# Issuing the attention scores of two key heads together, alternating between the lower and upper 64 rows

## The chip, the cores and the metric

The kernel runs on one core of one Trainium2 chip. Its metric is the device time of one execution in microseconds (us); lower is better. The program has two layers and is fully unrolled, so every instruction in the profile stands for one place in the code.

## The reference

A decoder trunk of two layers over 256 tokens and 2048 features, all in fp32. The part of a layer that the change touches is the attention half of its mixer: 16 query heads, 4 key heads of 64 features (four query heads share a key head), rotary positions, a window of 128 tokens and a sink value for each query head:

```python
q = rope(q.reshape(B, S, N_Q_HEADS, HEAD_DIM), positions)
k = rope(k.reshape(B, S, N_KV_HEADS, HEAD_DIM), positions)
...
# sliding_window_attention, blocks of 128 tokens, own and previous block as keys
scores = einsum('bnqhgd,bnkhd->bnhgqk', qb, kk) * HEAD_DIM ** -0.5
scores = where(valid, scores, MASK_VALUE)
m = maximum(max(scores, -1), sink)
e = exp(scores - m)
probs = e / (sum(e, -1) + exp(sink - m))
out = einsum('bnhgqk,bnkhd->bnqhgd', probs, vv)
```

Beside it a layer has a gated recurrence (the other half of the mixer), an output projection, a gated feed forward of width 5632 and a gated per-layer embedding. All big products are products of the 256 tokens with weight matrices that are read once.

## The kernel before, in words

The 256 tokens are two token tiles t = 0 and 1 of 128. A weight matrix is walked in strips of 512 output columns (`strip`), and a strip in chunks of 256 rows: `load_w` (lines 185 to 193) reads a chunk with one DMA and splits it into a high part (ScalarE, line 159) and a low part (VectorE, line 160). A chunk is then 12 matmuls of 512 columns on TensorE, six for each token tile (lines 206, 207, 208: high by high, low by high, high by low). They accumulate in four PSUM banks of their own (`pacc`). Split weights have eight buffers, so the splits can run up to eight chunks ahead of TensorE.

Everything smaller is threaded between the chunks. After each chunk `tick` advances the generators that are under way (one `yield` to the next) and runs what `later(n, ...)` had put off by n chunks. What is traced in this way is a program order; the framework's planner makes the order of each engine's queue from it, taking the earliest instruction of the program whose inputs are there by its own estimate of time. A queue then runs in that order on the chip. The small work shares four PSUM banks (`ms`, taken with `bank()`) and six buffers of 128x512 (`nat`).

A layer's mixer begins with the strip of keys and values. `done_kv` (line 404) rotates the keys: VectorE multiplies (line 395), GpSimd adds and subtracts (line 402), and TensorE transposes the result two or three chunks later (`turn`, line 414) into `kT`, whose lower 64 partitions hold the even key head of a half and the upper 64 the odd one. Then come two strips of queries, a half of the heads each. When a strip of queries is done, `attend` starts for each token tile, t = 1 one chunk behind t = 0: after three chunks the rotated queries are transposed (line 434), and from then on the two key heads g = 0 and 1 of the half go through `head_group` in three steps each, a chunk apart, with head 1 one chunk behind head 0:

- scores: a product over 64 rows (`rows = g * 64 ...`) for each of four query heads, line 464 for the own block and, for t = 1, line 472 for the block before; then the softmax up to its exponentials (lines 468 to 487, VectorE and ScalarE);
- the transposes of the exponentials (line 491) and their masks (lines 494 to 498);
- the products with the values (lines 503 and 505) and the division.

The attention of a half so runs during the next strip. That of half 1 runs during the first strip of the recurrence; at its end the outputs are scaled and transposed (`split_T`, lines 167, 175, 176), close to the first transposes of the recurrence (line 531).

Of the kernel before, what the change touches and what calls it, by code (L numbers as in the profile page):

```python
# [15 lines left out]
P = 128  # L16
# [23 lines left out]
BIG = (25600.0, 134.0, 1.921875, 0.005126953125, 1.6254460206255317e-05)  # 4096 * 2 pi  # L40
TWO = (6.28125, 0.0019350051879882812, 3.0199157663446385e-07)  # 2 pi
ROUND = 12582912.0  # 1.5 * 2^23
# [3 lines left out]
def decoder(ctx: ExitStack, tc: tile.TileContext, x, p, positions, w_in, attn_sinks,  # L46
# [23 lines left out]
    def later(n, fn):  # L70
        """trace fn n weight chunks from now"""
        queue.append((clock[0] + n, fn))
# [3 lines left out]
    def start(gen):  # L76
        """trace gen up to its first yield, and from one yield to the next every chunk"""
        running.append(gen)
        if next(gen, True):
            running.remove(gen)  # L80
# [17 lines left out]
    xr = [[xp.tile([P, W], F32, tag=f"x{t}{s}", name=f"x{t}{s}") for s in range(4)]  # L98
          for t in range(NT)]
# [6 lines left out]
    # per-feature vectors, one feature per partition  # L106
# [28 lines left out]
    def rstd(ss, n, count=1, name="rs"):  # L135
        """(ss / n + eps) ^ -0.5, ss [P, count]"""
        v = tiny(count)
        V.tensor_scalar(v, ss, 1.0 / n, EPS, op0=ALU.mult, op1=ALU.add)
        r = sm.tile([P, count], F32, name=name)
        G.tensor_tensor(r, v, mhalf[:, 0:count], op=ALU.pow)  # L140
        return r
# [15 lines left out]
    def split(src, hi, lo):  # L157
        """src = hi + lo, each of at most 12 significant bits"""
        S.copy(hi, src)  # L159
        V.tensor_tensor(lo, src, hi.bitcast(F32), op=ALU.subtract)  # L160

    def split_T(src_blocks, gcols, hl, t, kt0=0):
        """transpose 128-wide blocks [tok, feat] and split, per-feature gain if given"""
        n = len(src_blocks)
        ps = bank((P, n, P))
        for b, blk in enumerate(src_blocks):
            T.transpose(ps[:, b], blk, ident)  # L167
        h = hl[0][:, kt0:kt0 + n, t * P:(t + 1) * P]
        lo = hl[1][:, kt0:kt0 + n, t * P:(t + 1) * P]
        if gcols is None:  # L170
            split(ps, h, lo)
            return
        for b in range(n):
            g = gcols[:, b:b + 1]
            S.activation(h[:, b], ps[:, b], AF.Copy, scale=g)  # L175
            V.scalar_tensor_tensor(lo[:, b], ps[:, b], g, h[:, b].bitcast(F32),  # L176
                                   op0=ALU.mult, op1=ALU.subtract)
# [7 lines left out]
    def load_w(w, c, col):  # L185
        """two k-tiles of 512 columns, split"""
        raw = wpr.tile([P, 2, W], F32, tag="wr", name="wr")
        nc.sync.dma_start(raw, w[c * 2 * P:(c + 1) * 2 * P, col:col + W].rearrange(
            "(k p) n -> p k n", p=P))
        hi = wps.tile([P, 2, W], F32R, tag="wh", name="wh")  # L190
        lo = wps.tile([P, 2, W], F32R, tag="wl", name="wl")
        split(raw, hi, lo)
        return hi, lo

    def strip(lhs, w, col, done, nch=8, row0=0, skew=0, psum=None, pre=None):
        """512 output columns for both token tiles; lhs[c] = (hi, lo) of 4 k-tiles"""
# [31 lines left out]
    def post_norm(mg, ss, t, nss, xT, gcols):  # L228
        """after the last strip of a token tile: x += mg * rstd, and the next input"""
        r = sum_rstd(ss[t], D, f"po{t}")  # L230
        for c in range(4):
            V.scalar_tensor_tensor(xr[t][c], mg[c][:, t], r[:, 0:1], xr[t][c],  # L232
                                   op0=ALU.mult, op1=ALU.add)
            next_in(t, c, xT, gcols)
        for c in range(4):
            square_sum(xr[t][c], nss[t][:, c:c + 1])
# [16 lines left out]
    # ---- masks, sinks and rotary tables  # L253
    ones = cp.tile([P, P], F32, name="ones")
    m_low = cp.tile([P, P], F32, name="m_low")      # [j, i]: i >= j
    m_up = cp.tile([P, P], F32, name="m_up")        # [j, i]: i < j
    m_prev = cp.tile([P, P], F32, name="m_prev")    # [i, j]: j > i
    m_neg = cp.tile([P, P], F32, name="m_neg")      # [i, j]: j > i gives the mask value
    LEV = (1, 2, 4, 8, 16, 32, 64)  # block lengths; the last two take no mask
# [11 lines left out]
    def constants():  # L271
# [15 lines left out]
        # lower bounds: softmax over the layers, cumulative sum minus the first  # L287
# [22 lines left out]
        # attention sinks, on every partition  # L310
# [4 lines left out]
        # rotary angles: token per partition  # L315
# [52 lines left out]
    for l in range(DEPTH):  # L368
        # ================= mixer =======================================================
# [20 lines left out]
        def rotate(src, tb, i, n, o1, o2):  # L390
            """src [P, n heads, 64] in PSUM; o1, o2: [P, n/4, 4, 32] views in the order (g, j)"""
# [12 lines left out]
        def done_kv(t, ps):  # L404
# [11 lines left out]
            later(3 - t, turn)  # L416
# [12 lines left out]
        def attend(half, t, o):  # L429
# [7 lines left out]
            two = [head_group(half, g, t) for g in range(2)]  # L437
            next(two[0])
            yield
            next(two[1])  # L440
            next(two[0])
            yield
            next(two[1])
            next(two[0], None)
            yield
            next(two[1], None)
# [9 lines left out]
        def head_group(half, g, t):  # L456
            """four query heads on one key head: scores; then the exponentials' transpose; then values"""
            kv = 2 * half + g
            rows = slice(g * 64, (g + 1) * 64)
            q = qT[half]  # L460
            hs = slice(kv * 4, kv * 4 + 4)
            pc = bank((P, 4, P))
            for j in range(4):
                T.matmul(pc[:, j], q[rows, j, t * P:(t + 1) * P], kT[rows, half, t * P:(t + 1) * P],  # L464
                         start=True, stop=True)
            s_ = nat((P, 4, P))
            if t == 0:
                V.tensor_tensor(s_, pc, m_neg.unsqueeze(1).to_broadcast([P, 4, P]), op=ALU.add)
            else:
                pp = bank((P, 4, P))  # L470
                for j in range(4):
                    T.matmul(pp[:, j], q[rows, j, t * P:(t + 1) * P],
                             kT[rows, half, (t - 1) * P:t * P], start=True, stop=True)
                S.copy(s_, pc)
                V.copy_predicated(s_, m_prev.bitcast(I32).unsqueeze(1).to_broadcast([P, 4, P]), pp)
            nm = tiny(4)
            V.tensor_reduce(nm, s_, axis=AX.X, op=ALU.max, negate=True)
            V.tensor_tensor(nm, nm, nsink[:, l, hs], op=ALU.min)  # L478
            den = tiny(4)
            for j in range(4):  # L480
                S.activation(s_[:, j], s_[:, j], AF.Exp, bias=nm[:, j:j + 1],  # L481
                             accum_out=den[:, j:j + 1])
            es = tiny(4)
            V.tensor_tensor(es, sink[:, l, hs], nm, op=ALU.add)
            S.activation(es, es, AF.Exp)
            V.tensor_tensor(den, den, es, op=ALU.add)
            V.reciprocal(den, den)
            yield
            pt = bank((P, 4, P))
            for j in range(4):  # L490
                T.transpose(pt[:, j], s_[:, j], ident)  # L491
            ec = nat((P, 4, P))
            if t == 0:
                S.copy(ec, pt)
            else:
                ep = nat((P, 4, P))
                V.tensor_tensor(ec, pt, m_low.unsqueeze(1).to_broadcast([P, 4, P]), op=ALU.mult)
                V.tensor_tensor(ep, pt, m_up.unsqueeze(1).to_broadcast([P, 4, P]), op=ALU.mult)
            yield
            po = bank((P, 4, 64))  # L500
            for j in range(4):
                if t > 0:
                    T.matmul(po[:, j], ep[:, j], vv[:, t - 1, kv * 64:(kv + 1) * 64],
                             start=True, stop=False)
                T.matmul(po[:, j], ec[:, j], vv[:, t, kv * 64:(kv + 1) * 64],  # L505
                         start=t == 0, stop=True)
            dst = ao[t][:, half, g * 256:(g + 1) * 256]
            V.tensor_tensor(dst.rearrange("p (j d) -> p j d", d=64), po,
                            den.unsqueeze(2).to_broadcast([P, 4, 64]), op=ALU.mult)
            square_sum(dst, ssa[t][:, kv:kv + 1], (P, 256))  # L510

        class Rec:
            """four heads of the gated recurrence"""
# [151 lines left out]
        # ---- output projection, post norm  # L665
# [17 lines left out]
        # ================= feed forward ================================================  # L683
# [50 lines left out]
        # ================= gated per-layer embedding ===================================  # L734
# [61 lines left out]
```

## Time and profile before

| | |
|---|---|
| Time, median of 3 runs | 2515.0 us (2514.89 to 2515.26) |
| Span of the profiled execution | 2514.3 us |
| TensorE matmuls busy | 2490.2 us, 99% |
| TensorE weight loads busy | 2063.0 us, 82% |
| VectorE busy | 1431.4 us, 57% |
| ScalarE busy | 1179.4 us, 47% |
| GpSimd busy | 95.5 us, 4% |

No time of its own is given for the profiled execution beside its span; the span runs from its first to its last instruction and is 0.7 us below the median of the runs. In the profile PE is TensorE's matmuls, PEld its weight loads, DVE VectorE, ACT ScalarE and POOL GpSimd; `L464` is line 464 of the kernel. A row of the timeline gives start, length, engine, line, operation, the tile written and read, rows by columns of the stationary operand, the shape of the moving operand, and how many instructions are merged in the row. Matmuls are pipelined, so a row's length overlaps the next row's; the time an instruction takes from its neighbours is read from starts, not from lengths. A granted clock (PEclk) of 1.00 is TensorE's full speed.

### The profile page before, as it was taken

The page shows a single profiled execution, that of the slowest core. Times are in us where ns is not written, and L with a number is a line of the kernel's source. Part 1 is how long each engine was busy: PE and PEld are TensorE (multiplying, and loading weights), DVE is VectorE, ACT ScalarE, POOL GpSimd, SP SyncE. Part 2 cuts the span into 40 slices and gives each one's busy share as a digit, 9 for nine tenths or more (in the row PEclk, how much of TensorE's full clock was granted, in tenths as well). Part 3 has the DMA queues.
Part 4 walks back from the last instruction along what each step waited for, and adds up shares of the span by engine and source line. Part 5 has one row for each costly group of instructions (what it writes and reads, how often), then busy time and mean ns, then how long its engine had stood idle before and what let it go on. Part 6 is the DMA issues. An engine that isn't in the chain of part 4 may idle for free.

```text
span 2514.3 us, 31017 instructions
## 1 busy us (share of the span) xinstructions
PE 2490.2 (99%) x11779; PEld 2063.0 (82%) x11779; DVE 1431.4 (57%) x1777; ACT 1179.4 (47%) x1682; POOL 95.5 (4%) x209
## 2 busy tenths in 40 slices
PE   8999999999999999999999999999999999999999
PEld 6888888888888888887888888888888888888877
DVE  6666655544455455457566766565445544554574
ACT  6554445544444434446555443464444344344463
POOL 2100001000000000001011000010000000000010
PEclk9999999999999999999999999999999999999999
DMA  7344455656556656564563454556666665566653
GB/s 253 126 135 150 152 176 167 212 190 192 191 189 190 192 192 193 185 202 167 179 202 108 151 159 143 191 163 212 189 192 192 190 189 191 193 189 193 200 177 125
DMA packets 234260, 451.43 MB, mean 180 GB/s; under 512 B 14176, under 2 KB 15104, under 8 KB 234112
## 3 DMA queue, kind: packets, MB, share of 16 engines
q1 hardware_dynamic: 233808, 449.37, 55.9%
q8 instruction: 92, 1.51, 0.2%
q14 instruction: 56, 0.46, 0.0%
q10 hardware_dynamic: 240, 0.07, 0.0%
q0 software_dynamic: 64, 0.02, 0.0%
HBM read 447.31 MB, written 2.10 MB: 179 GB/s over the span
## 4 chain that ended last, share of the span: by engine, by line
PE 93%; ACT 2%; DVE 2%; DMA 1%; POOL 1%; issue 1%; SPq 0%; DVEq 0%; ACTq 0%; POOLq 0%
PE acc L206 29%; PE acc L208 29%; PE acc L207 29%; PE ms L579 1%; PE ms L167 1%; ACT junk L155 1%; PE ms L464 1%; ACT ck L175 1%; DVE wl L160 1%; ACT wh L159 1%; DMA wr<-in_w_in_dram 1%; PE ms L505 1%; DMA wr<-in_w_ple_gate_dram 0%; PE ms L594 0%; PE ms L491 0%
## 5 line engine op out<-in xcount | busy, mean ns | idle before, releaser
L160 DVE TENSOR_TENSOR wl<-wr,wh 128x1024 fp32r<-128x1024 f32 x840 | 1029.8, 1227 | 974.8 <-ACT wh L159 954.0
L159 ACT CAST wh<-wr 128x1024 fp32r<-128x1024 f32 x840 | 884.7, 1054 | 1189.2 <-PE acc L207 1127.0
L206 PE MATMUL acc<-wh,ck 128*128 128x512 f32 x3328 | 1309.2, 394 | 5.0 <-ACT ck L175 5.0
L208 PE MATMUL acc<-wl,ck 128*128 128x512 f32 x3328 | 1301.3, 391 | 0.4 <-DVE wl L160 0.4
L207 PE MATMUL acc<-wh,ck 128*128 128x512 f32 x3328 | 1299.9, 391 | 0.0
L206 PEld LDWEIGHTS acc<-wh,ck 128*128 128x128 f32 x3328 | 626.3, 188 | 134.0 <-ACT ck L175 7.6
L208 PEld LDWEIGHTS acc<-wl,ck 128*128 128x128 f32 x3328 | 625.9, 188 | 131.6 <-DVE wl L160 1.6
L207 PEld LDWEIGHTS acc<-wh,ck 128*128 128x128 f32 x3328 | 626.3, 188 | 126.3 <-DVE ck L160 0.5
L175 ACT ACTIVATE ck<-ms,gT 128x128 fp32r<-128x128 f32 x256 | 82.6, 379 | 30.8 <-DVE ck L176 26.1
L176 DVE SCALAR_TENSOR_TENSOR ck<-ms,gT,ck 128x128 fp32r<-128x128 f32 x256 | 79.0, 345 | 17.4 <-ACT ck L175 17.0
L145 POOL TENSOR_TENSOR tiny<-ssf 128x1 f32<-128x1 f32 x4 | 2.1, 534 | 1378.2 <-ACT junk L155 1377.9
L579 PEld LDWEIGHTS ms<-q,k 128*128 128x128 f32 x320 | 38.2, 191 | 2.7 <-PE acc L208 1.7
L579 PE MATMUL ms<-q,k 128*128 128x64 f32 x320 | 38.3, 272 | 0.0
L167 PE MATMUL ms<-ident,x 128*128 128x128 f32 x192 | 31.3, 287 | 5.1 <-DVE x L232 4.1
L697 ACT ACTIVATE nat<-acc,ry 128x512 f32<-128x512 f32 x44 | 30.2, 686 | 10.7 <-PE acc L208 10.6
L155 ACT ACTIVATE junk<-x 128x512 f32<-128x512 f32 x48 | 30.5, 636 | 9.2 <-DVE x L232 3.9
L167 PEld LDWEIGHTS ms<-ident,x 128*128 128x128 f32 x192 | 23.0, 146 | 14.4 <-issue 5.4
L723 DVE TENSOR_TENSOR macc<-acc,macc 128x512 f32<-128x512 f32 x48 | 33.0, 687 | 0.7
L703 DVE SCALAR_TENSOR_TENSOR nat<-acc,ry,nat 128x512 f32<-128x512 f32 x44 | 32.4, 748 | 0.1
L160 DVE TENSOR_TENSOR ck<-ms,ck 128x512 fp32r<-128x512 f32 x44 | 30.1, 684 | 0.0
L481 ACT ACTIVATE nat<-nat,tiny 128x128 f32<-128x128 f32 x64 | 24.9, 390 | 9.0 <-DVE tiny L478 9.0
L402 POOL TENSOR_TENSOR nat<-nat 128x256 f32<-128x256 f32 (+1 forms) x24 | 23.6, 1012 | 140.5 <-PE acc L208 77.9
(184 smaller groups left out, 889.6 us busy)
## 6 DMA issues: line engine op xcount, KB each, us to landing
wr<-in_w_in_dram SPq DMA_DIRECT2D x176, 512.0 KB, 3.5
wr<-in_w_ffn_gate_dram SPq DMA_DIRECT2D x176, 512.0 KB, 3.5
wr<-in_w_ffn_up_dram SPq DMA_DIRECT2D x176, 512.0 KB, 3.5
wr<-in_w_ffn_down_dram SPq DMA_DIRECT2D x176, 512.0 KB, 3.7
wr<-in_w_out_dram SPq DMA_DIRECT2D x64, 512.0 KB, 3.7
wr<-in_w_ple_gate_dram SPq DMA_DIRECT2D x64, 512.0 KB, 4.2
wr<-in_w_ple_proj_dram SPq DMA_DIRECT2D x8, 512.0 KB, 4.6
x<-in_x_dram SPq DMA_DIRECT2D x8, 256.0 KB, 5.3
```

The source lines that it names most:

```text
L155: S.activation(j[:, 0:shape[1]], src, AF.Square, accum_out=acc)
L159: S.copy(hi, src)
L160: V.tensor_tensor(lo, src, hi.bitcast(F32), op=ALU.subtract)
L167: T.transpose(ps[:, b], blk, ident)
L175: S.activation(h[:, b], ps[:, b], AF.Copy, scale=g)
L176: V.scalar_tensor_tensor(lo[:, b], ps[:, b], g, h[:, b].bitcast(F32), op0=ALU.mult, op1=ALU.subtract)
L206: T.matmul(ps[t], xh, hi[:, k], start=first, stop=False)
L207: T.matmul(ps[t], xl, hi[:, k], start=False, stop=False)
L208: T.matmul(ps[t], xh, lo[:, k], start=False, stop=last)
L579: T.matmul(pl[:, t * 4 + h].rearrange("p (b k) -> p b k", k=k), s.k[:, h, t * P:(t + 1) * P], up, start=True, stop=True)
L703: V.scalar_tensor_tensor(gate[t], ps, rx2(t)[:, 0:1], gate[t], op0=ALU.mult, op1=ALU.mult)
L723: V.tensor_tensor(m, ps, m, op=ALU.add)
```

## The change

The scores of both key heads of a half are issued in one step, all four banks at once for t = 1, with the heads alternating from product to product, so that neighbouring products use partitions 0 to 63 and 64 to 127 in turn. The softmax of head 0 is traced in that step and that of head 1 one chunk later. The transposes of the exponentials of head 0 follow two chunks after the scores, those of head 1 with the values of head 0 one chunk after that, and the values of head 1 last: five steps in place of four. In `done_kv` the transposes of the rotated keys are put off by two chunks more. Comments and docstrings are removed, with their lines left blank.

```diff
@@ done_kv
-            later(3 - t, turn)
+            later(5 - t, turn)
@@ attend
             yield
-            two = [head_group(half, g, t) for g in range(2)]
-            next(two[0])
-            yield
-            next(two[1])
-            next(two[0])
-            yield
-            next(two[1])
-            next(two[0], None)
-            yield
-            next(two[1], None)
+            yield from head_pair(half, t)
@@ scores
-            pc = bank((P, 4, P))
-            for j in range(4):
-                T.matmul(pc[:, j], q[rows, j, t * P:(t + 1) * P], kT[rows, half, t * P:(t + 1) * P],
-                         start=True, stop=True)
...
+            blocks = [t] if t == 0 else [t, t - 1]
+            sc = {}
+            for u in blocks:
+                for g in range(2):
+                    sc[u, g] = bank((P, 4, P))
+                for j in range(4):
+                    for g in range(2):
+                        rows = slice(g * 64, (g + 1) * 64)
+                        T.matmul(sc[u, g][:, j], q[rows, j, t * P:(t + 1) * P],
+                                 kT[rows, half, u * P:(u + 1) * P], start=True, stop=True)
+            ex, dens = [], []
+            for g in range(2):
...            # softmax of head g as before, from sc[t, g] and sc[t - 1, g]
+                ex.append(s_)
+                dens.append(den)
+                if g == 0:
+                    yield
             yield
...            # turned(g): transposes and masks of head g; values(g, parts): as before
+            p0 = turned(0)
+            yield
+            p1 = turned(1)
+            values(0, p0)
+            yield
+            values(1, p1)
```

More of the change, by code (lines that the diff above doesn't have):

```diff
@@ L454, in attend, with head_pair @@
                     split_T(blocks4(ao[t][:, h]), gain_cols(96, l, 8)[:, 4 * h:4 * h + 4], attn[h], t)
-        def head_group(half, g, t):
-            kv = 2 * half + g
-            rows = slice(g * 64, (g + 1) * 64)
+        def head_pair(half, t):
             q = qT[half]
-            hs = slice(kv * 4, kv * 4 + 4)
-            pc = bank((P, 4, P))
-            for j in range(4):
-                T.matmul(pc[:, j], q[rows, j, t * P:(t + 1) * P], kT[rows, half, t * P:(t + 1) * P],
-                         start=True, stop=True)
[L466 to L470, printed above, removed]
-                for j in range(4):
[L472 to L487, printed above, removed]
-            yield
[L489 to L495, printed above, removed]
@@ new lines, in head_pair @@
+            for g in range(2):
+                kv = 2 * half + g
+                hs = slice(kv * 4, kv * 4 + 4)
+                s_ = nat((P, 4, P))
+                if t == 0:
+                    V.tensor_tensor(s_, sc[t, g], m_neg.unsqueeze(1).to_broadcast([P, 4, P]),
+                                    op=ALU.add)
+                else:
+                    S.copy(s_, sc[t, g])
+                    V.copy_predicated(s_, m_prev.bitcast(I32).unsqueeze(1).to_broadcast([P, 4, P]),
+                                      sc[t - 1, g])
+                nm = tiny(4)
+                V.tensor_reduce(nm, s_, axis=AX.X, op=ALU.max, negate=True)
+                V.tensor_tensor(nm, nm, nsink[:, l, hs], op=ALU.min)
+                den = tiny(4)
+                for j in range(4):
+                    S.activation(s_[:, j], s_[:, j], AF.Exp, bias=nm[:, j:j + 1],
+                                 accum_out=den[:, j:j + 1])
+                es = tiny(4)
+                V.tensor_tensor(es, sink[:, l, hs], nm, op=ALU.add)
+                S.activation(es, es, AF.Exp)
+                V.tensor_tensor(den, den, es, op=ALU.add)
+                V.reciprocal(den, den)
+                ex.append(s_)
+                dens.append(den)
+                if g == 0:
+                    yield
@@ L496, in head_group, with turned @@
+            yield
+            def turned(g):
+                pt = bank((P, 4, P))
+                for j in range(4):
+                    T.transpose(pt[:, j], ex[g][:, j], ident)
+                ec = nat((P, 4, P))
+                if t == 0:
+                    S.copy(ec, pt)
+                    return [(t, ec)]
                 ep = nat((P, 4, P))
@@ L498, in head_group, with values @@
                 V.tensor_tensor(ep, pt, m_up.unsqueeze(1).to_broadcast([P, 4, P]), op=ALU.mult)
-            yield
[L500 to L510, printed above, removed]
+                return [(t - 1, ep), (t, ec)]
+            def values(g, parts):
+                kv = 2 * half + g
+                po = bank((P, 4, 64))
+                for j in range(4):
+                    for i, (u, e) in enumerate(parts):
+                        T.matmul(po[:, j], e[:, j], vv[:, u, kv * 64:(kv + 1) * 64],
+                                 start=i == 0, stop=i == len(parts) - 1)
+                dst = ao[t][:, half, g * 256:(g + 1) * 256]
+                V.tensor_tensor(dst.rearrange("p (j d) -> p j d", d=64), po,
+                                dens[g].unsqueeze(2).to_broadcast([P, 4, 64]), op=ALU.mult)
+                square_sum(dst, ssa[t][:, kv:kv + 1], (P, 256))
+            p0 = turned(0)
+            yield
+            p1 = turned(1)
+            values(0, p0)
+            yield
+            values(1, p1)
         class Rec:
```

## The prediction

> **What bounds the kernel now.** I read the page first, then the groups of the score lines, then TensorE's timeline around the attention of the first half, then single stretches of it with their clock.
>
> ```profile
> span 2514.3 us, 31017 instructions
> ...
> PE 2490.2 (99%) x11779; PEld 2063.0 (82%) x11779; DVE 1431.4 (57%) x1777; ACT 1179.4 (47%) x1682; POOL 95.5 (4%) x209
> ...
> PE 93%; ACT 2%; DVE 2%; DMA 1%; POOL 1%; issue 1%; SPq 0%; DVEq 0%; ACTq 0%; POOLq 0%
> ...
> L464 PE MATMUL ms<-kT,qT x128: 272/272/373, 73.8 to 1372.4; 64*128 64x128 f32 x128
> ...
> L472 PE MATMUL ms<-kT,qT x64: 272/272/373, 82.6 to 1373.3; 64*128 64x128 f32 x64
> ```
>
> TensorE is busy all the time and makes 93% of the chain that ends last. So a change pays by what it takes out of, or adds to, TensorE's queue, and by waits in it; VectorE and ScalarE have slack. The scores are 128 + 64 = 192 instructions. The code has 96 score products, so each is two instructions of the same 64 rows. The timeline of half 0 in layer 0:
>
> ```profile
> 73.49 0.39 PE L208 MATMUL acc<-wl,ck 128*128 128x512 f32 x1
> 73.81 1.16 PE L464 MATMUL ms<-kT,qT 64*128 64x128 f32 x8
> 74.89 0.66 PE L434 MATMUL ms<-ident,nat 128*128 128x128 f32 x4
> ...
> 77.92 0.39 PE L208 MATMUL acc<-wl,ck 128*128 128x512 f32 x1
> 78.23 1.16 PE L464 MATMUL ms<-kT,qT 64*128 64x128 f32 x8
> 79.32 0.50 PE L206 MATMUL acc<-wh,ck 128*128 128x512 f32 x1
> 79.66 0.39 PE L207 MATMUL acc<-wh,ck 128*128 128x512 f32 x1
> 79.89 0.39 PE L208 MATMUL acc<-wl,ck 128*128 128x512 f32 x1
> 80.12 0.27 PE L491 MATMUL ms<-ident,nat 128*128 128x128 f32 x1
> 80.32 0.49 PE L464 MATMUL ms<-kT,qT 64*128 64x128 f32 x2
> 80.74 0.33 PE L491 MATMUL ms<-ident,nat 128*128 128x128 f32 x1
> 81.00 0.48 PE L464 MATMUL ms<-kT,qT 64*128 64x128 f32 x2
> 81.41 0.33 PE L491 MATMUL ms<-ident,nat 128*128 128x128 f32 x1
> 81.67 0.71 PE L464 MATMUL ms<-kT,qT 64*128 64x128 f32 x4
> 82.31 0.33 PE L491 MATMUL ms<-ident,nat 128*128 128x128 f32 x1
> 82.57 1.16 PE L472 MATMUL ms<-kT,qT 64*128 64x128 f32 x8
> 83.65 0.65 PE L206 MATMUL acc<-wh,ck 128*128 128x512 f32 x1
> ...
> 88.77 1.16 PE L464 MATMUL ms<-kT,qT 64*128 64x128 f32 x8
> 89.76 1.05 PE L472 MATMUL ms<-kT,qT 64*128 64x128 f32 x8
> ...
> 1371.49 1.16 PE L464 MATMUL ms<-kT,qT 64*128 64x128 f32 x8
> ```
>
> Two prices are to be seen. Inside a block a score costs (1.05 - 0.272) / 7 = 0.11 us (row 89.76, whose 8 follow 8 others; 0.112 in what follows). Around a block there is a border: from 77.92 to 79.66 are 1.74 us, of which a weight matmul before and one after take 0.23 each (79.66 to 79.89) and 8 scores 0.90, so the border costs 0.39 us. Followed by transposes it is 0.34 (73.49 to 74.89: 1.40 - 0.23 - 0.90 = 0.28, and 0.06 in the transposes behind). In the stretch from 80.12 to 83.65 four single transposes cut 16 scores into four blocks: 3.53 - 4 x 0.11 - 16 x 0.112 = 1.3 us, 0.32 each, and 0.11 behind the last. A layer has 7 blocks in half 0 (the rows above) and 4 in half 1, 22 in all, the first at 73.81 and the last at 1371.49. At some 0.36 each their borders take 7.9 us, and the bodies 192 x 0.112 = 21.5 us.
>
> The same stretch has a second cost:
>
> ```profile
> 79.89:83.65 3.76, 3.76 (x22) 2.63 (x20) 2.93 (x9) 3.76 (x17) 0.00 (x0) 1.00 0.00 0
> 83.65:87.40 3.75, 3.75 (x10) 2.92 (x10) 0.75 (x2) 0.59 (x3) 0.00 (x0) 0.54 0.44 144
> ...
> 1331.21:1333.39 2.18, 2.18 (x11) 1.75 (x11) 0.73 (x1) 0.51 (x2) 0.00 (x0) 1.00 0.76 240
> ```
>
> After 3.5 us of scores and transposes without one weight matmul the granted clock falls to 0.54, and the same 9 weight matmuls take 3.75 us where layer 1, at clock 1.00, takes 2.18: 1.57 us lost. Layer 1 has the same stretch in front of it and loses nothing, so it is a matter of where the stretch falls.
>
> **The change part by part.** Borders. t = 0 makes one block of 16 per half and t = 1 one of 32: 8 blocks, 4 followed by the transposes of the queries (0.34) and 4 by weights (0.39), 2.9 us. Gain 7.9 - 2.9 = 5.0 us. The new program order puts no transposes of exponentials beside the scores of t = 1 (they come a chunk later), so nothing is there to cut the block.
>
> Bodies. No row of this trace shows neighbouring products on different halves of the array. Bounds: each half alone keeps its pace of 0.112 and the two run side by side, 0.056 per instruction, gain 10.75 us; or the second half waits as the same half does, 0.112, gain 0; a loss is the rival below. Inside the gain, the instructions are lower, lower, upper, upper, and matmuls start in order: the second lower one waits 0.112 for the first, the first upper one follows it closely, and so on, one wait for every two. The closest that two different matmuls follow each other here is 0.03 us:
>
> ```profile
> 92.01 0.27 PE L491 MATMUL ms<-ident,nat 128*128 128x128 f32 x1
> 92.04 0.48 PE L208 MATMUL acc<-wl,ck 128*128 128x512 f32 x1
> ```
>
> That makes (0.112 + 0.03) / 2 = 0.07 the slow end of side by side, gain 8.1 us. I take the middle of 0.056 and 0.07, 0.063: 192 x 0.049 = 9.4 us. Why side by side rather than 0.112: the two products share neither partitions nor, each head having its own tile, a PSUM bank, and the 0.112 is what one half needs for 128 columns.
>
> The Trainium skill bears on it ("TensorE: Matmul & The Clock Gate", Part 3, The mechanism): matmuls in different row groups are said to start about 4 ns apart and to overlap, and weight loads for a row group that is free are pulled ahead. By that rule the bodies would cost 0.058 and the time would be 2498.0 us; no run here shows it yet. The same page (What overlaps and what doesn't) says that a load overlaps a matmul in flight only in another row group. This trace differs: with loads of 0.19 us the same 64 rows still go at 0.112, so the starting point is twice as good as that rule would have it.
>
> Clock. The longest stretch without weights becomes 32 scores, 32 x 0.063 = 2.0 us in place of 3.5, and both halves of the array work in it. I count the 1.57 us of layer 0 as gone, and let it stay in the range.
>
> Softmax, masks, values. The same instructions, one chunk (2.7 us of weights) later for the second half of them. VectorE and ScalarE run behind TensorE only in stretches like 79.89:83.65 above (ScalarE 3.76 of 3.76); the eight buffers of split weights cover that, and transposes now come one chunk after the exponentials at the earliest. Cost 0. If the cover were gone, a bank would be late next: t = 1 now takes all four `ms` banks at once, and its second one is free only when the softmax of t = 0, head 1, has read its scores. The only wait of that kind in the region is in front of line 531:
>
> ```profile
> 148.16 0.66 PE L531 MATMUL ms<-ident,nat 128*128 128x128 f32 x4 [0.86 <-DVE ck L176]
> ```
>
> The last `split_T` pairs of half 1 move one chunk towards line 531, so that both of its transposes now share a chunk with one; the wait of 0.86 us may go or double in each layer: -1.7 to +1.7 us, taken as 0. A wait like it before each of the four blocks of t = 1 would cost up to 3.4 us; taken as 0.
>
> Transposes of the keys. They are where TensorE stands still in layer 0:
>
> ```profile
> 53.70 0.69 PE L414 MATMUL ms<-ident,nat 128*128 128x128 f32 x2 [2.88 <-POOL nat L402]
> 54.04 0.78 PE L206 MATMUL acc<-wh,ck 128*128 128x512 f32 x1
> 54.61 0.63 PE L207 MATMUL acc<-wh,ck 128*128 128x512 f32 x1
> 55.04 0.63 PE L208 MATMUL acc<-wl,ck 128*128 128x512 f32 x1
> ...
> 57.12 0.38 PE L414 MATMUL ms<-ident,nat 128*128 128x128 f32 x2
> ...
> L206 PE MATMUL acc<-wh,ck 128*128 128x512 f32 x50 | 20.3, 423 | 4.6 <-ACT ck L175 4.6
> ```
>
> TensorE waits 2.88 us for GpSimd and then runs slow weight matmuls, 0.57 and 0.43 us apart in place of 0.23; at six of them, an estimate, that is 0.34 + 4 x 0.2 + 0.1 for the last, 1.2 us more. But 50 matmuls of line 206, so 50 x 3 = 150 weight matmuls, stand before the first transpose. By the program order before it was due after the 8 chunks of keys and values and 2 of the next strip, 10 x 12 = 120. The planner has put it off to 150, in the middle of a chunk, because by its own estimate the keys were not ready before. Two chunks more make it due at 144, still before 150: it will stand where it stands. Gain 0; if it does move, 2.88 + 1.2 = 4.1 us. In layer 1 there is no such wait to win.
>
> Sum: 5.0 + 9.4 + 1.6 = 16.0 us. The span goes from 2514.3 to 2498.3, and with the 0.7 us by which the median of the runs, 2515.0, lies above it the time is 2499.0 us. I take 0.2%, 5 us, as what a measurement of this kernel can tell from no change.
>
> **The rivals.** First: the halves do not run side by side. In TensorE's rows a weight load starts with the matmul before it, never ahead of it:
>
> ```profile
> 123.67 0.19 PEld L208 LDWEIGHTS acc<-wl,ck 128*128 128x128 f32 x1
> 123.89 0.40 PE L208 MATMUL acc<-wl,ck 128*128 128x512 f32 x1
> 123.89 0.59 PEld L491 LDWEIGHTS ms<-ident,nat 128*128 128x128 f32 x4
> ```
>
> If that also holds across halves, the upper load can start only when the second lower matmul has started, and four instructions take two loads and two matmuls in turn, about 0.11 each: gain 0 in the bodies. For it: the rows. Against it: in all of them the load goes where weights wait already, so it could not have started earlier. What is left is 5.0 us, and the block of 32 scores is then 3.6 us long, as long as the stretch that cost a clock step. With none, one, two or all four blocks hit the time is 2515.0 - 5.0 + (n - 1) x 1.57 us: 2508.4, 2510.0, 2511.6, 2514.7.
>
> Second, the other side: every change of half costs. A border holds about 0.09 us for emptying the array, 0.10 for a first load that nothing hides, and 0.09 on the way out. There are 7 + 15 changes of half for each attention half, 88 in all. At 0.19 us each (emptying and load) they cost 16.7 us, less 5.0: 2526.7 us. It is slower than before from 5.0 / 88 = 0.057 us, and by over 0.2% from 0.114. Against it: in an alternation the other half is free to be loaded meanwhile.
>
> Third: the keys' transposes do move. With the main case 2494.9 us.
>
> **How the numbers follow.** Side by side 0.52 (2495 to 2505 by the bounds 0.056 to 0.07, clock step or not, bank waits of up to 3.4 us); that and moved keys 0.08; not side by side 0.30; a cost at every change of half 0.07; longer waits 0.03. Faster by over 0.2%, below 2510: the first two and one third of the third, 0.70. Same: most of the rest of the third, 0.20. Slower: 0.10. The range reaches from moved keys, 2494, to two clock steps, 2512.
>
> **What would show it.** Right: line numbers of the scores in 8 unbroken blocks, 32 of them within about 2.1 us, clock 1.00 behind the blocks, the wait in front of the keys' transposes still near 2.9 us. Wrong: blocks of 32 that take 3.5 us or more (rivals one and two), single transposes or weights inside them, a wait on a bank in front of them, or more than 150 weight matmuls ahead of the first transposes of the keys.

## The result and the profile after

The changed kernel takes 2500.2 us (median of its runs, 2499.2 to 2501.0) where the kernel before took 2515.1 us on the same chip: a ratio of 0.9934, interval 0.9922 to 0.9946, so 15.0 us or 0.6% faster. The prediction was 2499.0 us. The profiled execution has a span of 2498.6 us, 15.7 less than before; the prediction's sum gave 2498.3. First, from the page, its span, the busy times and the chain that ended last:

```profile
span 2498.6 us, 31016 instructions
...
PE 2473.7 (99%) x11779; PEld 2049.7 (82%) x11779; DVE 1429.7 (57%) x1777; ACT 1177.8 (47%) x1682; POOL 91.9 (4%) x209
...
PE 92%; ACT 3%; DVE 2%; DMA 1%; issue 1%; POOL 1%; SPq 0%; DVEq 0%; ACTq 0%; POOLq 0%
```

TensorE has as many instructions as before and is busy for 16.5 us less. ScalarE's part of the chain has risen from 2% to 3%; that comes back below. TensorE's timeline of the attention of layer 0, half 0 and then, from 112 us, half 1 (start, length, engine, line; the idle time before an instruction and what ended it stand in brackets):

```profile
73.58 1.16 PE L458 MATMUL ms<-kT,qT 64*128 64x128 f32 x16
74.67 0.66 PE L434 MATMUL ms<-ident,nat 128*128 128x128 f32 x4
...
78.01 2.06 PE L458 MATMUL ms<-kT,qT 64*128 64x128 f32 x32
80.00 0.50 PE L206 MATMUL acc<-wh,ck 128*128 128x512 f32 x1
80.33 0.39 PE L207 MATMUL acc<-wh,ck 128*128 128x512 f32 x1
...
82.62 0.39 PE L208 MATMUL acc<-wl,ck 128*128 128x512 f32 x1
83.07 0.66 PE L493 MATMUL ms<-ident,nat 128*128 128x128 f32 x4
...
86.75 1.00 PE L508 MATMUL ms<-vv,nat 128*128 128x64 f32 x8
88.03 0.66 PE L493 MATMUL ms<-ident,nat 128*128 128x128 f32 x4 [0.27 <-ACT nat L469]
...
112.10 2.06 PE L458 MATMUL ms<-kT,qT 64*128 64x128 f32 x32
...
120.13 0.60 PE L493 MATMUL ms<-ident,nat 128*128 128x128 f32 x4
121.09 1.10 PE L508 MATMUL ms<-vv,nat 128*128 128x64 f32 x8 [0.37 <-ACT nat L496]
```

All scores now have one line, 458, and stand in unbroken blocks of 16 and 32, eight in all with layer 1. The 32 take 1.99 us from their first start to the next weight matmul (78.01 to 80.00), the prediction had "about 2.1"; the 32 instructions of before at 0.112 would have taken 3.6 us. Behind them, after 0.33 for the first, the weight matmuls follow at 0.23 to 0.24 us: there is no slow stretch. How the scores follow each other is seen where only line 458 is counted in a very short window:

```profile
73.57:73.60 0.03, 0.02 (x2) 0.03 (x2) 1.00 1.07 410
```

Two score matmuls and two weight loads are under way in the first 0.03 us of the block. Taken one by one, their starts come in pairs: 7 ns within a pair and, after a first gap of some 206 ns, 105 ns to the next pair, 0.112 us for two instructions or 0.056 for one. The rows do not name the half that an instruction works on; that a pair has one of each follows from the run below with all scores on the lower rows, where no two start closer than 0.111 us. So both halves of the array keep the pace of 0.112 that one half had alone.

Where the time came from is read by comparing the same pieces of TensorE's queue. Each window below begins where a fixed number of weight matmuls have run (216 and 312 in layer 0, 5256 and 5352 in layer 1) and ends 72 weight matmuls later, so it holds one half's attention. Before:

```profile
70.89:104.46 33.57, 33.57 (x191) 27.86 (x190) 19.84 (x40) 18.93 (x58) 0.00 (x0) 0.95 0.35 110
110.26:141.80 31.54, 31.54 (x200) 27.16 (x198) 18.93 (x40) 19.08 (x58) 3.01 (x8) 1.00 0.37 117
1318.45:1350.45 32.00, 32.00 (x191) 26.69 (x189) 19.83 (x40) 18.87 (x58) 0.00 (x0) 1.00 0.38 117
1356.25:1387.79 31.54, 31.54 (x200) 27.16 (x198) 18.94 (x40) 19.08 (x58) 2.99 (x8) 1.00 0.38 119
```

After:

```profile
70.66:98.82 28.16, 27.83 (x191) 23.50 (x189) 19.80 (x40) 19.05 (x56) 1.40 (x2) 1.00 0.45 139
104.75:132.78 28.03, 27.66 (x191) 23.54 (x190) 19.41 (x40) 19.10 (x57) 1.59 (x5) 1.00 0.40 116
1310.14:1338.26 28.12, 27.84 (x192) 23.50 (x190) 19.81 (x40) 18.99 (x56) 1.40 (x2) 1.00 0.46 139
1344.19:1372.22 28.03, 27.66 (x192) 23.53 (x190) 19.43 (x40) 19.08 (x57) 1.58 (x5) 1.00 0.41 115
```

The first figure is the length, the next TensorE's busy time, and the third from the end the granted clock. The four pieces sum to 128.65 us before and 112.34 after, 16.31 less, so the whole gain lies here and the rest of the program gives 0.6 back, in this pair of profiles. In half 1 some of it is only moved: 8 transposes of `split_T`, 0.8 us in each layer, now come behind the window (200 instructions of TensorE before, 191 after). Two more things are to be seen. The clock of the first piece was 0.95 and is 1.00. And TensorE, which before was busy for the whole of each piece, now stands still for 0.3 to 0.4 us in each: waits that the kernel before did not have.

### The profile page after: what moved, and what is told of

Its sections match the earlier page's. It is cut to its first block, busy times and chain, and to the rows that moved or that the text cites. A ratio compares the mean times of both kernels' runs of the same rounds, so it can differ in the third digit from the quotient of the medians.

```text
span 2498.6 us, 31016 instructions
## 1 busy us (share of the span) xinstructions
PE 2473.7 (99%) x11779; PEld 2049.7 (82%) x11779; DVE 1429.7 (57%) x1777; ACT 1177.8 (47%) x1682; POOL 91.9 (4%) x209
## 4 chain that ended last, share of the span: by engine, by line
PE 92%; ACT 3%; DVE 2%; DMA 1%; issue 1%; POOL 1%; SPq 0%; DVEq 0%; ACTq 0%; POOLq 0%
PE acc L206 29%; PE acc L208 29%; PE acc L207 29%; PE ms L167 1%; PE ms L589 1%; PE ms L508 1%; ACT junk L155 1%; DVE wl L160 1%; ACT wh L159 1%; DMA wr<-in_w_in_dram 1%; ACT ck L175 1%; ACT nat L477 1%; DMA wr<-in_w_ple_gate_dram 0%; PE ms L604 0%; DVE x L232 0%
## 5 line engine op out<-in xcount | busy, mean ns | idle before, releaser
L707 ACT ACTIVATE nat<-acc,ry 128x512 f32<-128x512 f32 x44 | 30.2, 686 | 10.7 <-PE acc L208 10.7
```

## The experiments

The first four ran on one chip with the kernel before at 2517.4 us, the other four on another with the kernel before at 2517.2. All times are compared on their own chip. The changed kernel itself was not run on the second one; there the kernel with the keys' transposes at their old place stands for it.

**The changed kernel again.** No edit; it gives the level for the three that follow.

> The changed kernel once more, so that the others of this chip have it beside them. 2500.2 us, 0.993 to 0.995 of the kernel before; 8 score blocks with pairs of starts 0.007 and 0.105 us apart.

Measured: 2500.4 us (2498.9 to 2502.9), ratio 0.9936 (0.9922 to 0.9949), span 2498.2.

**Both heads on the lower 64 rows.** It has all of the new order, but nothing to run side by side. Head 1's own products are left out; those of head 0's rows stand in their place.

```diff
-                        rows = slice(g * 64, (g + 1) * 64)
+                        rows = slice(0, 64)
```

> The changed kernel with the scores of head 1 taken from rows 0 to 63 as well (the keys and queries of head 0, so head 1's scores are left out); the order, the banks and the blocks stay. Theory, two halves of the array side by side: starts 0.112 us apart again, 192 x 0.056 = 10.75 us more than the changed kernel, 2510.9 us, and up to four clock steps of 1.57 us on top, since a block of 32 is then 3.6 us of one half only. Rival, the gain came from fewer borders, or from neighbouring products going to different PSUM banks: no change, 2500.2 us.

Measured: 2508.5 us, ratio 0.9966 (0.9953 to 0.9978). The block of 32 scores in its timeline, and two of its four pieces:

```profile
78.97 3.83 PE L458 MATMUL ms<-kT,qT 64*128 64x128 f32 x32
82.73 0.50 PE L206 MATMUL acc<-wh,ck 128*128 128x512 f32 x1
```

```profile
70.70:100.79 30.09, 30.09 (x191) 26.18 (x190) 20.00 (x40) 19.25 (x56) 1.40 (x2) 1.00 0.44 129
1349.97:1380.03 30.06, 30.06 (x191) 26.18 (x190) 19.45 (x40) 19.19 (x57) 2.68 (x5) 1.00 0.37 109
```

The block takes 3.76 us in place of 1.99, with one start every 0.112. So running side by side is what makes the bodies short. End to end that is worth 8.2 us and not the 10.7 that the score instructions alone show, and the rows say why: TensorE is busy for all of each piece (30.09 of 30.09), so the new waits are gone here. With slower scores the softmax is in time. The run also shows the borders by themselves: against the kernel before its four pieces are 8.4 us shorter, of which 1.6 are the clock step of layer 0, 1.6 the moved transposes, and 5.2 the borders.

It bears on a point of the first rival, too. That rival let the clock fall behind blocks of 3.6 us; these blocks are that long, and in all four pieces of the profiled execution the clock is 1.00.

**Heads one after the other, not alternating.** Eight instructions of the lower half, then eight of the upper.

```diff
-                for j in range(4):
-                    for g in range(2):
+                for g in range(2):
+                    for j in range(4):
```

> The changed kernel with the two heads after one another in each block of keys (four products of the lower half, then four of the upper) in place of alternating. If passes start strictly in order, only the last pass of one half and the first of the next overlap, 16 changes of half x 0.105 us: 10.75 - 1.7 = 9.1 us more, 2509.3 us. If the next product may overtake, but only that one: 4 + 12 of 96 products are paired rather than all, 7.2 us more, 2507.4 us. If each half has a queue of its own: no change, 2500.2 us. Either way the borders are those of the changed kernel, so what is left against the kernel before, 6 to 8 us, is borders and the clock.

Measured: 2503.7 us (2502.9 to 2504.3), ratio 0.9946 (0.9933 to 0.9958).

```profile
79.95 2.82 PE L458 MATMUL ms<-kT,qT 64*128 64x128 f32 x32
82.70 0.50 PE L206 MATMUL acc<-wh,ck 128*128 128x512 f32 x1
```

The block takes 2.75 us, between the two cases, and none of the expected times came. The single starts of its first instructions lie 214, 111, 112, 112, 6, 105, 108, 4 ns apart. By the count, these are four lower ones alone, then a lower and an upper one 6 ns apart, though a lower product and a half still stand between them in the program. The planner did not move them: in the program built from this kernel TensorE's queue has the score instructions as written, eight lower and then eight upper. TensorE therefore does not start matmuls strictly in program order; work for a free half is brought forward over the waiting ones, but not from any distance, or the upper half would have started at once. The score instructions cost 5.2 us more than with alternation, the kernel 3.3.

**Two and two.** Lower, lower, upper, upper products.

```diff
-                for j in range(4):
-                    for g in range(2):
+                for j, g in ((0, 0), (1, 0), (0, 1), (1, 1), (2, 0), (3, 0), (2, 1), (3, 1)):
```

> The changed kernel with two products of the lower half, then two of the upper. If the next product alone may overtake: every block begins and ends with one product alone, 0.22 us more in each of 8 blocks, 1.8 us more than the changed kernel, 2502.0 us, and pairs in between. If only the passes of the products next to each other in the program mix: about half of the gain is lost, 5 us more. If each half has a queue of its own: no change.

Measured: 2501.1 us (2497.6 to 2502.1), ratio 0.9933 (0.9921 to 0.9946): as the changed kernel.

```profile
75.61 2.16 PE L458 MATMUL ms<-kT,qT 64*128 64x128 f32 x32
77.69 0.50 PE L206 MATMUL acc<-wh,ck 128*128 128x512 f32 x1
```

2.08 us for the block in place of 1.99. The pairs begin with the first instruction (13 ns apart), so the first upper product overtakes a whole lower product. In this run and in the one before, the first upper instruction starts beside the lower one that stands four places ahead of it in the queue, and not beside one five places ahead. Strict alternation is not needed for the time; it is enough that the other half's work stands within about two products.

That the times are equal hides two differences. The score instructions take 0.8 us longer than with strict alternation, and yet the four pieces sum to 111.66 us in place of 112.34, because in half 1 TensorE no longer waits. Its piece of layer 0:

```profile
102.23:129.95 27.72, 27.72 (x192) 23.74 (x190) 19.35 (x40) 19.09 (x57) 1.59 (x5) 1.00 0.41 117
```

**The keys' transposes at their old place.** This undoes the second part of the change alone.

```diff
-            later(5 - t, turn)
+            later(3 - t, turn)
```

> The changed kernel with the transposes of the keys at their old place in the program (3 - t chunks). Theory: this part of the change does nothing; in layer 0 they stand behind 150 weight matmuls in either, with the wait of 2 to 3.4 us on GpSimd in front, and layer 1 has no wait: 2500.3 us, ratio to the kernel before 0.993 to 0.995. Rival: the two chunks more were worth something, 1 to 4 us slower.

Measured: 2501.1 us (2499.2 to 2503.6), ratio 0.9935 (0.9922 to 0.9947), which is that of the changed kernel. **Three chunks later still:**

```diff
-            later(5 - t, turn)
+            later(8 - t, turn)
```

> The changed kernel with those transposes five chunks later than the kernel before has them (8 - t), due behind 180 weight matmuls, where the planner's estimate no longer decides. Theory: the wait on GpSimd and the slow clock behind it go; the stretch from weight matmul 120 to 216 takes 22.4 us instead of the 26.3 to 27.8 us of the changed kernel's profiles, 4 to 5 us less, 2496 us. Rival: the time comes back as a wait for the rotated queries or the scores: 2500.3 us.

Measured: 2497.5 us (2496.6 to 2498.2), ratio 0.9920 (0.9907 to 0.9934). The first of these transposes in the changed kernel:

```profile
53.16 0.44 PE L414 MATMUL ms<-ident,nat 128*128 128x128 f32 x2 [3.31 <-POOL nat L402]
```

With the old place:

```profile
54.16 0.69 PE L414 MATMUL ms<-ident,nat 128*128 128x128 f32 x2 [2.31 <-POOL nat L402]
```

And three chunks later, with the stretch from the 120th to the 216th weight matmul that holds it:

```profile
58.43 0.60 PE L414 MATMUL ms<-ident,nat 128*128 128x128 f32 x4
```

```profile
44.83:67.41 22.58, 22.58 (x105) 18.70 (x104) 19.02 (x35) 13.62 (x18) 8.56 (x8) 1.00 0.82 256
```

In the first two kernels 150 weight matmuls stand ahead of the transposes, as in the kernel before, and TensorE waits for GpSimd. The two chunks of the change move only layer 1's transposes, which waited for nothing. Put off by five chunks they are at last past the planner's own place, the wait is gone and the stretch takes 22.58 us, where the changed kernel takes:

```profile
42.88:70.66 27.78, 24.46 (x106) 19.74 (x104) 19.19 (x35) 13.83 (x18) 8.52 (x8) 0.94 0.69 208
```

And in its second run, with the clock at 1.00:

```profile
43.31:69.63 26.32, 22.88 (x106) 18.59 (x104) 19.17 (x35) 13.76 (x18) 8.52 (x8) 1.00 0.74 219
```

In all eight profiles that have the transposes behind 150 weight matmuls, the stretch takes 24.81 to 27.78 us; with the old place, on the same chip, 26.73. Of the 4.1 us between that and 22.58, 3.7 arrive at the end (the two kernels' ranges on that chip do not meet).

**Copies of the scores ahead of the exponentials.** The scores of both heads leave PSUM before the first exponential, to take away the wait for line 469.

```diff
+            raw = []
             for g in range(2):
                 s_ = nat((P, 4, P))
...              # mask (t = 0) or copy and mask (t = 1), as before
+                raw.append(s_)
+            ex, dens = [], []
+            for g in range(2):
+                s_ = raw[g]
                 nm = tiny(4)
```

> The changed kernel with the scores of both heads copied out of their banks before the first exponential, so that ScalarE's copy of head 1 no longer stands behind head 0's exponentials. Theory: the new waits in the attention (on line 469's copy, half 0) come from there; the two halves 0, 28.2 and 28.1 us from weight matmul to weight matmul, lose 0.5 to 0.7 us each, half 1's wait on line 496 stays: 2499 us. Rival: ScalarE is full in that stretch whatever the order: no change, 2500.3 us.

Measured: 2500.8 us (2498.8 to 2502.7), ratio 0.9933 (0.9920 to 0.9945): no gain. Its pieces of half 0 and half 1 in layer 0, and TensorE's row with the wait (line 508 is 512 here, 496 is 500):

```profile
68.22:96.27 28.05, 27.94 (x192) 23.33 (x190) 19.51 (x40) 19.03 (x56) 1.41 (x2) 1.00 0.47 143
102.20:130.40 28.20, 27.67 (x191) 23.54 (x190) 19.14 (x40) 18.98 (x57) 1.56 (x5) 1.00 0.44 131
```

```profile
118.73 1.10 PE L512 MATMUL ms<-vv,nat 128*128 128x64 f32 x8 [0.53 <-ACT nat L500]
```

Half 0 is 0.11 us shorter and half 1 0.17 longer: the wait only changed its place. The rival's reason, a full ScalarE, does not hold in half 1 either. In the changed kernel ScalarE stands idle there for 2.08 us ahead of the exponentials, until VectorE has the row maximum (lines 473 and 474), and VectorE makes the low part of a weight chunk (line 160) first:

```profile
116.78 1.23 DVE L160 TENSOR_TENSOR wl<-wr,wh 128x1024 fp32r<-128x1024 f32 x1 [0.21 <-ACT wh L159]
117.92 0.68 DVE L473 TENSOR_REDUCE tiny<-nat 128x4 f32<-128x512 f32 x1
...
118.83 0.40 ACT L477 ACTIVATE nat<-nat,tiny 128x128 f32<-128x128 f32 x1 [2.08 <-DVE tiny L474]
```

With two and two the planner has these two the other way round, and half 1 has no wait:

```profile
114.08 0.69 DVE L473 TENSOR_REDUCE tiny<-nat 128x4 f32<-128x512 f32 x1
114.68 1.21 DVE L160 TENSOR_TENSOR wl<-wr,wh 128x1024 fp32r<-128x1024 f32 x1
```

The exponentials there start 6.33 us after the block of 32 scores does, 0.4 earlier than the 6.73 of the changed kernel, and the wait was 0.37. So VectorE's order has a part in the waits; no run moved line 160 alone.

**Both: copies first and the keys' transposes three chunks later.**

> Both of these in one kernel. Theory: the two are far apart in time, so the sum, 2494.5 us; faster than the kernel before by 0.8%.

Measured: 2497.1 us (2496.3 to 2498.8), ratio 0.9917 (0.9904 to 0.9931). Not to be told from the kernel with the later transposes alone. The ranges of both lie below those of the kernel before and of the kernel with the old place; the version to keep is the simpler one, `later(8 - t, turn)` and nothing else: 19.7 us below the kernel before.

## Why the prediction was right

The mechanism was the one forecast, and the total came within 1.2 us of the median and 0.3 us of the span. That closeness is in part luck: two terms were too small and two costs were left out, and they cancel. The span is not known to 0.3 us either: up to the 120th weight matmul, ahead of all that the change touches, the ten profiles take from 42.88 to 45.65 us. Term by term, in us of gain; the measured column is read from the starts of TensorE's instructions in the three kernels before, both heads on the lower rows, and after:

| step | predicted | measured |
|---|---|---|
| borders of 22 blocks become 8 | 5.0 | 5.2 |
| bodies, 192 instructions from 0.112 down | 9.4 | 10.7 |
| clock step in layer 0 | 1.6 | 1.6 |
| wait in front of line 531 | 0 | 2.1 |
| new waits in the attention | 0 | -2.7 |
| keys' transposes | 0 | -0.7 |
| rest of the program | 0 | -0.4 |
| sum | 16.0 | 15.8 |

**Borders** were priced from rows and held. **Bodies**: the prediction took 0.063 us an instruction, between 0.056 and 0.07, because it let matmuls start in order and each product's two instructions stand together. That step was wrong. The lower and upper instructions of two products interleave from the first pair on, and the two orders without strict alternation show upper products starting ahead of lower ones. The fast end of the range, 0.056, is what runs. The Trainium skill ("TensorE: Matmul & The Clock Gate", Part 3, The mechanism) lets matmuls of different row groups start about 4 ns apart and pulls weights ahead for a free row group; the 6 to 7 ns of the pairs are close to it. Where the same page of the Trainium skill lets a load overlap a matmul in flight only in another row group (What overlaps and what doesn't), the runs still differ: with all scores on the same 64 rows they go at 0.112 us with loads of 0.19.

**New waits** were named ("a bank would be late next", up to 3.4 us in front of the score blocks of t = 1) and taken as nothing. None came in front of those blocks; they came at the transposes of the exponentials and the products with the values, and cost 2.7 us. The cover that the prediction gave for them, softmax running behind TensorE only in the stretches of single transposes, was counted in TensorE's slow time. Shorter score blocks leave the softmax less of it. In the window ahead of the transposes at 83.07 ScalarE is busy without a gap (the fourth busy time):

```profile
80.00:83.07 3.07, 3.01 (x14) 2.17 (x13) 0.70 (x5) 3.07 (x17) 0.00 (x0) 1.00 0.02 6
```

And the timeline of VectorE and ScalarE ahead of the row at 88.03:

```profile
84.44 1.22 DVE L160 TENSOR_TENSOR wl<-wr,wh 128x1024 fp32r<-128x1024 f32 x1
85.57 0.15 DVE L474 TENSOR_TENSOR tiny<-tiny,nsink 128x4 f32<-128x4 f32 x1
...
85.76 0.40 ACT L477 ACTIVATE nat<-nat,tiny 128x128 f32<-128x128 f32 x1 [0.36 <-DVE tiny L474]
...
87.41 0.56 ACT L469 COPY nat<-ms 128x512 f32<-128x512 f32 x1
```

The copy that frees the bank (line 469) stands behind another head's exponentials and ends at 87.97, and TensorE goes on at 88.03. Those exponentials in turn began 0.36 us late, because VectorE made the low part of a weight chunk (line 160) ahead of line 474. The brackets give only idle time; the drain and the load that nothing hides add to it: from 86.75 to 88.03 are 1.28 us where the same 8 products with the values otherwise take 0.83, and from 82.62 to 83.07 0.45 in place of 0.23. That is 0.67 in this half, 2.7 if all four are alike; the pieces of the same-rows run give the same 2.7 (7.9 us of difference where the score instructions alone make 10.7). This is the price that the same-rows experiment got back and that moving the copies could not.

**The wait in front of line 531** (0.86 us before, bounds -1.7 to +1.7, taken as 0) went in both layers; with what lies around it, it is the 2.1 us above. **The keys' transposes** stayed behind 150 weight matmuls, as argued. The -0.7 of the table is the stretch from the 120th to the 216th weight matmul, 27.78 us after and, before:

```profile
43.86:70.89 27.03, 24.15 (x106) 19.63 (x104) 19.03 (x35) 13.72 (x18) 8.51 (x8) 0.94 0.67 219
```

Since that stretch varies by 3 us over the eight profiles that leave the transposes there, it says nothing about the change; the experiment with the old place shows that this part of the change does nothing, and the one with the later place that the price named for moving them, 4.1 us, was about right (3.7).

**The rest of the program** was not in the sum at all. Its -0.4 is made up of 1.0 gained before the 120th weight matmul, where nothing was changed, 0.9 lost at the transposes of the per-layer embedding in layer 0, and 0.5 lost in small steps. The 0.9 can be seen. Before, after, and with the keys' transposes three chunks later (line 756 before is 766 after):

```profile
1195.76 0.66 PE L167 MATMUL ms<-ident,x 128*128 128x128 f32 x4 [0.55 <-DVE x L756]
```

```profile
1187.46 0.66 PE L167 MATMUL ms<-ident,x 128*128 128x128 f32 x4 [1.43 <-DVE x L766]
```

```profile
1184.68 0.66 PE L167 MATMUL ms<-ident,x 128*128 128x128 f32 x4 [1.83 <-DVE x L766]
```

The earlier TensorE gets there, the longer it waits. What it waits for (line 766, 756 before) stands in VectorE's queue behind the low part of a chunk, and that behind ScalarE's high part, which now waits for the weights to arrive; before, and after:

```profile
1192.74 1.05 ACT L159 CAST wh<-wr 128x1024 fp32r<-128x1024 f32 x1
```

```profile
1184.51 1.05 ACT L159 CAST wh<-wr 128x1024 fp32r<-128x1024 f32 x1 [0.83 <-DMA wr<-in_w_ple_gate_dram]
```

So 0.9 us of the gain seems to be given back to a weight stream that does not come earlier by as much. That this stream is the limit there is read from the rows; no run tested it.

**The rivals.** Not side by side: out by the paired starts. A price for each change of half: out, since blocks with a change at every step are the shortest of all that were run. The keys' transposes move: out, though it is worth what was said once it is made to happen.

## What to carry to other kernels

Products over 64 rows are worth ordering so that lower and upper ones stand within about two products of each other: they then cost half, 0.056 in place of 0.112 us an instruction here, and of the orders run, strict alternation took the least time in the scores themselves, though not end to end. A gain on the bounding engine uncovers what ran in its shadow, so the cover that a term of zero leans on has to be recounted with the shorter stretch; here that took 2.7 us. What stands in a helper engine's queue ahead of small work counts in this: one weight split of 1.2 us ahead of a row maximum went with a wait on TensorE that the other order did not have. And a move in program order does nothing while the planner's own estimate puts the instruction later anyway: look up where it stands in the queue, and move it past that place or not at all.

## What was not expected of the hardware

TensorE does not keep program order between the halves of its array: with four lower products ahead of four upper ones, the upper half began beside the fifth lower instruction, 6 ns behind it. How far it looks ahead is bounded by the orders run here, not measured exactly. The clock step stays open. In the kernel before it came behind 3.5 us without weight matmuls in layer 0 and not behind the same stretch in layer 1; blocks of 3.76 us on one half, four in one execution, did not bring it, so neither the length nor the use of one half alone explains it. All nine profiles of the new order show 1.00 in all four pieces; of the kernel before there is one profile, so how often it takes the step is not known, and the 1.6 us of the table rest on that one. The same holds for the slow stretch at the keys' transposes: the changed kernel showed a clock of 0.94 there in one execution and 1.00 in another.
